# One change to a two-layer decoder trunk: where the third pooling group is multiplied, who adds and splits, and how the first and the down-projection loads are issued

## The chip, the cores and the metric

The kernel runs on one core of a Trainium2 chip. A core has a matrix engine (TensorE, PE in the profile, with its weight loads as PEld), a vector engine (VectorE, DVE), a scalar engine (ScalarE, ACT), GpSimd (POOL) and a queue that only issues loads and stores (SyncE, SP). They share an on-chip memory of 128 partitions, and TensorE's accumulation banks, of which this kernel uses eight of 128x512 float32. The metric is the device time of one execution in microseconds (us).

## The reference, cut to what matters

Two layers, 512 tokens, width 1024. Layer 0 mixes tokens by dilated attention, layer 1 by pooling; each is followed by a SwiGLU feed-forward network of width 2816, with a root-mean-square norm ahead of every part.

```python
def pooling_mixer(h, w_in, w_group, scale):
    u = (h @ w_in).reshape(B, S, POOL_GROUPS, POOL_GROUP_DIM)
    ys = [trailing_mean(u[:, :, g], w) - u[:, :, g] for g, w in enumerate(POOL_WINDOWS)]  # 2, 4, 8, 16
    y = jnp.einsum('bsgc,gcd->bsgd', jnp.stack(ys, axis=2), w_group).reshape(B, S, D_MODEL)
    return y * scale

def swiglu_ffn(h, w_gate_up, w_down):
    gu = h @ w_gate_up
    return (jax.nn.silu(gu[..., :D_FF]) * gu[..., D_FF:]) @ w_down

x = x + dilated_attention_mixer(rmsnorm(x, attn_norm), w_qkv, w_attn_out)
x = x + swiglu_ffn(rmsnorm(x, ffn_norm[0]), w_gate_up[0], w_down[0])
x = x + pooling_mixer(rmsnorm(x, pool_norm), w_pool_in, w_pool_group, pool_scale)
x = x + swiglu_ffn(rmsnorm(x, ffn_norm[1]), w_gate_up[1], w_down[1])
return rmsnorm(x, final_norm)
```

## The kernel before, in words

Activations lie transposed: X[0] to X[7] are eight tiles of 128 channels by 512 tokens. To keep float32 accuracy at TensorE's faster rate, every operand is split into a high half (a rounded copy) and a low half (the rest), and a product is three matmuls per chunk of 128 channels: high by high, high by low, low by high (lines 321, 322 and 324 for plain products; 453 to 455 in the seven-product scheme for 2x2 blocks that most of the work uses).

Weights stream through a ring of raw buffers. A plan that is written out ahead (lines 235 to 276) fixes the order of loads and splits, and `pump` works it off, behind each product. A plain weight unit is split in one of two ways (line 135). Either ScalarE makes the high half and VectorE subtracts (lines 91 and 92), or, if the unit is called `lean`, ScalarE makes the high half (L139) and its negation (L140), and GpSimd's queue adds the weights onto it by a second, accumulating load (L143). The first part (two chunks of the hidden width, `first == 0`) and the last part (four chunks) of each down projection are lean units of several pieces, each with a load of its own for every output chunk (L132 and L143).

The start (lines 887 to 919): the norms' weights are loaded, six warm-up matmuls on zeros run (L894, twelve passes in the profile), and for every chunk k of the input, X[k] (L902) and the first weights (L903) are loaded by SP, scaled and split (L383 or L385, L386; L908 or L906, L910), and multiplied in twelve matmuls (L914).

The pooling stage (lines 1219 to 1275) has four groups g of two chunks each. `pool(g)` takes two projections from TensorE, and on VectorE evacuates each (L1231), builds the window's sum (L1237 or L1241), subtracts (L1246, L1248) and splits the result (L91 on ScalarE, L92 on VectorE). `mix(g)` multiplies the two chunks by the group's weights in two products of six matmuls, adds the result to X (L1257), makes the next stage's operand (high half L385 on ScalarE, low half L386 on VectorE), squares X on ScalarE (L374) and adds the squares on GpSimd (L376). The order is pool 3, pool 2, mix 3, pool 1, mix 2, pool 0, mix 1, then the first products of the feed-forward network on chunks 4 to 7, then mix 0. Each projection is begun two calls ahead of its evacuation, so the last two are on TensorE while pool 1 is evacuated. Each engine works its own instructions strictly in the order in which they stand.

Of the kernel before, what the change touches and what calls it, by code (L numbers as in the profile page):

```python
# [9 lines left out]
F32R = mybir.dt.float32r  # L10
AF = mybir.ActivationFunctionType
OP = mybir.AluOpType
# [3 lines left out]
P = 128  # L16
# [20 lines left out]
NF = 4  # L37
H2 = S // 2
K2 = KC // 2
NPLAIN = 4  # L40
WARM = 6
NSOLO = 3
# [22 lines left out]
def trunk(ctx: ExitStack, tc: tile.TileContext, xT, xN, norms, w_first, w_qk, w_qkp, w_v0, w_v0p, w_v12, w_out, w_pair, w_down, w_dblock, w_pin, w_pgrp,  # L65
          consts, ident_in, invcnt_in, outT, outR):
    nc = tc.nc
# [52 lines left out]
    class Plain:  # L120


        def __init__(self, *srcs, shift=0, lean=False):
            self.srcs, self.n, self.w, self.shift, self.lean = srcs, sum(src.shape[-1] for src in srcs), None, shift, lean
            loads.append((self, {"raw": 1}, self.load))
            steps.append((self, "w", self.split))

        def load(self):
            self.raw = Held("raw")
            o = 0  # L130
            for src in self.srcs:
                nc.sync.dma_start(self.raw.t[:, o:o + src.shape[-1]], src)  # L132
                o += src.shape[-1]

        def split(self):
            self.w = Held("w", self.shift)
            hi, lo = (t[:, :self.n] for t in self.w.t)
            if self.lean:
                nc.scalar.activation(hi, self.raw.t[:, :self.n], AF.Copy)  # L139
                nc.scalar.activation(lo, hi.bitcast(F32), AF.Copy, scale=-1.0)  # L140
                o = 0
                for src in self.srcs:
                    nc.gpsimd.dma_start(lo[:, o:o + src.shape[-1]], src.bitcast(F32R), accum_op=OP.add)  # L143
                    o += src.shape[-1]
            else:
                split(hi, lo, self.raw.t[:, :self.n])
            self.raw.done()
# [103 lines left out]
    def ffn_plan(layer):  # L251
        j = 0
        for i, (first, end, block) in enumerate(PARTS):
# [10 lines left out]
            else:  # L264
                sizes = units_of(end - first)
                step = D // (sizes[0] * P) if len(sizes) == 1 else 1
                for m in range(0, KC, step):
                    o = first * P
                    for n in sizes:
                        share(step, *[w_down[layer, q, :, o:o + n * P] for q in range(m, m + step)], lean=True,  # L270
                              shift=LINE // 4 * (layer == 1 and end == FC and m + step > KC - ENDS))
                        o += n * P
# [86 lines left out]
    def give(key):  # L359
        del taken[held.pop(key)]  # L360
# [231 lines left out]
    with tc.tile_pool(name="opool", bufs=1) as opool:  # L592
        early = opool.tile([P, HEADS, S], F32R, tag="o", name="early")
        with tc.tile_pool(name="apool", bufs=1) as apool:
# [291 lines left out]

            nc.sync.dma_start(nrm, norms)
            lead = [Product(KC, stream(0), w=(None, None)) for i in range(NF)]
# [6 lines left out]
            for k in range(KC):  # L895
# [6 lines left out]
                nc.sync.dma_start(X[k], xT[:, k, :])  # L902
                nc.sync.dma_start(raw[:, s], w_first[k])  # L903
                if k:
                    scaled(0, k, *U[k])
                    nc.scalar.activation(hi[:, s], raw[:, s], AF.Copy)  # L906
                else:
                    nc.scalar.activation(hi[:, s], raw[:, s], AF.Copy)  # L908
                    scaled(0, k, *U[k], on_dve=True)
# [109 lines left out]
    with tc.tile_pool(name="fpool", bufs=2) as fpool:  # L1019
# [202 lines left out]

        def pool(g):
            Y[g] = []
            for c in range(2):
                left = KC - 2 * len(Y) - c + 2
                lead.extend(begin(min(left, 3) - len(lead), 2, range(KC)))
# [23 lines left out]
                split(*Y[g][-1], y)  # L1251

        def mix(g):
            for c in range(2):
                f = Product(2, lambda k: Y[g][k], w=wg[g // 2, g % 2]).add(range(2), pos=2 * c)
                m = 2 * g + c
# [3 lines left out]
                scaled(3, m, t[:, 0], t[:, 1])  # L1260
                square(3, m, nc.gpsimd)
            for c in range(2):
                give(("y", g, c))

        pool(3)
        pool(2)
        mix(3)
        pool(1)
        mix(2)
# [189 lines left out]
```

## Time and profile before

| | before |
|---|---|
| median of 3 runs | 1192.59 us (1192.28 to 1192.77) |
| the profiled execution's own time | 1192.39 us |
| its span in the profile | 1190.6 us |
| mean granted TensorE clock | 0.999 |
| moved from and to memory | 207.30 MB |

A row of the timeline has the start (us from the span's start), the duration, the engine, the line, the operation, what it writes and reads, how many alike are merged (x), and in brackets how long the engine had been idle and what ended that. A matmul's row runs to the end of its way through the array, so neighbouring rows overlap: what counts is the distance of two starts. A row of the waits names who waited, for whom, and three numbers: the total, how often, the longest.

### The profile page before, as it was taken

To read this page: it belongs to the slowest core of one execution; us is meant where nothing else is said; L and a number is where in the kernel's file an instruction comes from. 1 tells how busy PE (TensorE), PEld (TensorE's weight loads), DVE (VectorE), ACT (ScalarE), POOL (GpSimd) and SP (SyncE) were. 2 spreads that over 40 slices of the span, in tenths; PEclk is the share of its full clock that TensorE was granted. 3 is DMA by queue.
4 is the path that set the end of the run, shared out by engine and by line. 5 is a ranking of instruction groups with operands and counts; after the bars stand their busy time and mean duration, and the time that the engine had idled before them with its cause. 6 is when DMAs were issued, how large, how long until landed. Compare 5 with 4: busy or idle time off the path is not lost.

```text
span 1190.6 us, 24964 instructions
## 1 busy us (share of the span) xinstructions
PE 1180.9 (99%) x9936; PEld 1119.4 (94%) x9936; DVE 961.6 (81%) x1682; ACT 715.1 (60%) x1247; POOL 201.8 (17%) x201
## 2 busy tenths in 40 slices
PE   9999999999999999999999999999999999999997
PEld 7889999999999988889999999988789999999997
DVE  6978798889788854699988988657779998898855
ACT  6445564455456545747756776676575776676563
POOL 1111211111111002411111111122450111111120
PEclk9999999999999999999999999999999999999999
DMA  8346666665766548957777777798595777777763
GB/s 276 127 102 164 155 155 162 170 158 149 191 144 163 155 141 209 196 105 200 191 191 192 195 201 195 192 265 206 116 196 112 192 196 200 193 192 195 194 135 96
DMA packets 83733, 207.30 MB, mean 174 GB/s; under 512 B 8464, under 2 KB 13728, under 8 KB 83616
## 3 DMA queue, kind: packets, MB, share of 16 engines
q1 hardware_dynamic: 51552, 141.98, 36.3%
q0 software_dynamic: 31920, 63.46, 32.3%
q8 instruction: 78, 1.28, 0.4%
q14 instruction: 39, 0.32, 0.1%
q10 hardware_dynamic: 144, 0.26, 0.1%
HBM read 203.57 MB, written 2.10 MB: 173 GB/s over the span
## 4 chain that ended last, share of the span: by engine, by line
PE 97%; issue 1%; DVE 1%; ACT 1%; POOL 0%; DVEq 0%; POOLq 0%
PE ps L453 19%; PE ps L455 19%; PE ps L454 19%; PE ps L321 8%; PE ps L322 8%; PE ps L324 8%; PE ps L624 2%; PE ps L626 2%; PE ps L625 2%; PE ps L914 2%; PE ps L836 1%; PE ps L708 1%; PE ps L830 1%; PE ps L728 1%; PE ps L894 0%
## 5 line engine op out<-in xcount | busy, mean ns | idle before, releaser
L91 ACT ACTIVATE w<-raw 128x1024 fp32r<-128x1024 f32 x261 | 276.2, 1063 | 169.5 <-PE ps L455 71.8
L92 DVE TENSOR_TENSOR w<-raw,w 128x1024 fp32r<-128x1024 f32 x261 | 317.8, 1221 | 50.0 <-ACT w L91 46.0
L453 PE MATMUL ps<-far,w 128*128 128x256 f32 x896 | 246.7, 275 | 0.5 <-ACT first L527 0.5
L454 PE MATMUL ps<-far,w 128*128 128x256 f32 x896 | 246.5, 275 | 0.0
L455 PE MATMUL ps<-far,w 128*128 128x256 f32 x896 | 246.5, 275 | 0.0
L453 PE MATMUL ps<-near,w 128*128 128x256 f32 x640 | 180.3, 282 | 0.0
L454 PE MATMUL ps<-near,w 128*128 128x256 f32 x640 | 177.0, 277 | 0.0
L455 PE MATMUL ps<-near,w 128*128 128x256 f32 x640 | 176.9, 276 | 0.0
L453 PEld LDWEIGHTS ps<-far,w 128*128 128x128 f32 x896 | 168.2, 188 | 1.0 <-ACT first L527 0.9
L454 PEld LDWEIGHTS ps<-far,w 128*128 128x128 f32 x896 | 168.2, 188 | 0.1
L455 PEld LDWEIGHTS ps<-far,w 128*128 128x128 f32 x896 | 168.2, 188 | 0.0
L322 PE MATMUL ps<-near,w 128*128 128x512 f32 (+1 forms) x332 | 125.0, 377 | 1.3 <-DVE near L386 1.3
L321 PE MATMUL ps<-near,w 128*128 128x512 f32 (+1 forms) x332 | 125.6, 379 | 0.0
L324 PE MATMUL ps<-near,w 128*128 128x512 f32 (+1 forms) x332 | 124.9, 376 | 0.0
L453 PEld LDWEIGHTS ps<-near,w 128*128 128x128 f32 x640 | 120.5, 188 | 0.4
L454 PEld LDWEIGHTS ps<-near,w 128*128 128x128 f32 x640 | 120.3, 188 | 0.0
L455 PEld LDWEIGHTS ps<-near,w 128*128 128x128 f32 x640 | 120.3, 188 | 0.0
L168 POOL DMA_DIRECT2D raw<-w_pair x36 | 43.5, 1208 | 296.0 <-DMA raw<-w_pair 113.6
L322 PEld LDWEIGHTS ps<-near,w 128*128 128x128 f32 x332 | 62.4, 188 | 12.9 <-DVE near L386 1.7
L321 PEld LDWEIGHTS ps<-near,w 128*128 128x128 f32 x332 | 62.3, 188 | 11.7 <-ACT near L91 0.4
L324 PEld LDWEIGHTS ps<-near,w 128*128 128x128 f32 x332 | 62.3, 188 | 11.5
L139 ACT ACTIVATE w<-raw 128x1024 fp32r<-128x1024 f32 x36 | 37.8, 1056 | 37.4 <-PE ps L324 35.4
(311 smaller groups left out, 2813.1 us busy)
## 6 DMA issues: line engine op xcount, KB each, us to landing
raw<-w_pair SPq DMA_DIRECT2D x80, 512.0 KB, 4.9
raw<-w_qkp SPq DMA_DIRECT2D x36, 512.0 KB, 4.4
raw<-w_pair POOLq DMA_DIRECT2D x36, 512.0 KB, 7.5
raw<-w_dblock SPq DMA_DIRECT2D x32, 512.0 KB, 4.6
raw<-w_v SPq DMA_DIRECT2D x18, 512.0 KB, 4.3
raw<-w_qkp POOLq DMA_DIRECT2D x18, 512.0 KB, 7.5
rawhalf<-w_pair SPq DMA_DIRECT2D x36, 256.0 KB, 5.1
raw<-w_dblock POOLq DMA_DIRECT2D x16, 512.0 KB, 7.4
```

The source lines that it names most:

```text
L91: nc.scalar.activation(hi, v, AF.Copy)
L92: nc.vector.tensor_tensor(lo, v, hi.bitcast(F32), op=OP.subtract)
L139: nc.scalar.activation(hi, self.raw.t[:, :self.n], AF.Copy)
L168: nc.gpsimd.dma_start(self.b.rearrange("p (a c) -> p a c", a=2), self.src[:, None, 3 * n:].to_broadcast([P, 2, n]), accum_op=OP.add)
L321: nc.tensor.matmul(self.p[:, cols], w[0][:, s], mh[:, cols], start=self.done == 0, stop=False)
L322: nc.tensor.matmul(self.p[:, cols], w[0][:, s], ml[:, cols], start=False, stop=False)
L324: nc.tensor.matmul(self.p[:, cols], w[1][:, s], mh[:, cols], start=False, stop=self.done == self.n)
L453: nc.tensor.matmul(dst, w.t[0][:, c], th, start=k == 0 and not on, stop=False, skip_group_check=on)
L454: nc.tensor.matmul(dst, w.t[0][:, c], tl, start=False, stop=False, skip_group_check=on)
L455: nc.tensor.matmul(dst, w.t[1][:, c], th, start=False, stop=k == n - 1, skip_group_check=on)
L624: nc.tensor.matmul(o, mh, wh, start=k == 0, stop=False)
L625: nc.tensor.matmul(o, mh, wl, start=False, stop=False)
```

## The change

- At the start the norms are loaded by GpSimd's queue, four warm-up matmuls run instead of six, X[0] is SP's first load, and the first weights of chunk 0 come in two halves, each with a copy of its own on ScalarE.
- Units of several pieces are loaded by one transfer: four pieces of 256 columns or two of 512. The last part of layer 1's down projection is no longer lean: VectorE subtracts, and the accumulating loads there go.
- The two products of the pooling group g=2 are issued inside pool 1, between the last two projections; the rest of mix 2 follows pool 1 as before.
- In `mix` the squares are added by VectorE, both behind the two chunks' operands.

```diff
-WARM = 6
+WARM = 4
...
+        def views(self, t):
+            o = 0
+            for src in self.srcs:
+                q = src.shape[1] if len(src.shape) == 3 else 1
+                v = t[:, o:o + q * src.shape[-1]]
+                yield v.rearrange("p (q c) -> p q c", q=q) if len(src.shape) == 3 else v, src
+                o += q * src.shape[-1]
...
-                        share(step, *[w_down[layer, q, :, o:o + n * P] for q in range(m, m + step)], lean=True,
+                        share(step, w_down[layer, m:m + step, :, o:o + n * P].rearrange("q p c -> p q c"), lean=layer == 0 or first == 0,
...
-            nc.sync.dma_start(nrm, norms)
+            nc.gpsimd.dma_start(nrm, norms)
...
                 nc.sync.dma_start(X[k], xT[:, k, :])
-                nc.sync.dma_start(raw[:, s], w_first[k])
                 if k:
+                    nc.sync.dma_start(raw[:, s], w_first[k])
                     scaled(0, k, *U[k])
                     nc.scalar.activation(hi[:, s], raw[:, s], AF.Copy)
                 else:
-                    nc.scalar.activation(hi[:, s], raw[:, s], AF.Copy)
+                    for e in range(2):
+                        c = slice(e * NF * P // 2, (e + 1) * NF * P // 2)
+                        nc.sync.dma_start(raw[:, c], w_first[k][:, c])
+                        nc.scalar.activation(hi[:, c], raw[:, c], AF.Copy)
                     scaled(0, k, *U[k], on_dve=True)
...
-        def pool(g):
+        def pool(g, inside=None):
             Y[g] = []
             for c in range(2):
+                if inside and c:
+                    inside()
...
+        M = {}
+
+        def mixed(g):
+            M[g] = [Product(2, lambda k: Y[g][k], w=wg[g // 2, g % 2]).add(range(2), pos=2 * c) for c in range(2)]
+
         def mix(g):
-            for c in range(2):
-                f = Product(2, lambda k: Y[g][k], w=wg[g // 2, g % 2]).add(range(2), pos=2 * c)
+            if g not in M:
+                mixed(g)
+            for c, f in enumerate(M.pop(g)):
...
-                square(3, m, nc.gpsimd)
             for c in range(2):
+                square(3, 2 * g + c)
                 give(("y", g, c))
...
-        pool(1)
+        pool(1, lambda: mixed(2))
```

The first place is VectorE's program in the pooling stage, before the change, from the evacuation of the last projection on (`s_` with a number is a running sum, `x` the residual, `near` the next stage's operand, `far` a split pooled chunk):

```order
L1231 TENSOR_TENSOR u<-ps,row 128x512
L1237 TENSOR_TENSOR s_10273<-u 128x512
L1257 SCALAR_TENSOR_TENSOR x<-ps,nrm,x 128x512
L1244 TENSOR_TENSOR mean<-s_10273,invcnt 128x2
L1246 SCALAR_TENSOR_TENSOR u<-s_10273,u 128x510
L1257 SCALAR_TENSOR_TENSOR x<-ps,nrm,x 128x512
L386 SCALAR_TENSOR_TENSOR near<-x,nrm,near 128x512
L92 TENSOR_TENSOR far<-u,far 128x512
L386 SCALAR_TENSOR_TENSOR near<-x,nrm,near 128x512
```

After the change, from the evacuation of the last projection but one on (the changed file's lines 1240, 1246, 1253, 1255, 1257, 1272, 390 and 380 are lines 1231, 1237, 1244, 1246, 1248, 1257, 386 and 376 of before):

```order
L1240 TENSOR_TENSOR u<-ps,row 128x512
L1246 TENSOR_TENSOR s_10238<-u 128x512
L1272 SCALAR_TENSOR_TENSOR x<-ps,nrm,x 128x512
L1253 TENSOR_TENSOR mean<-s_10238,invcnt 128x2
L1255 SCALAR_TENSOR_TENSOR u<-s_10238,u 128x510
L1272 SCALAR_TENSOR_TENSOR x<-ps,nrm,x 128x512
L390 SCALAR_TENSOR_TENSOR near<-x,nrm,near 128x512
L380 TENSOR_TENSOR sq<-sq 128x512
L390 SCALAR_TENSOR_TENSOR near<-x,nrm,near 128x512
L380 TENSOR_TENSOR sq<-sq 128x512
L1257 TENSOR_TENSOR u<-mean,u 128x2
L92 TENSOR_TENSOR far<-u,far 128x512
```

The same chain of g=2 has moved from behind the last evacuation to behind the one before it, and two additions of squares stand in it.

The second place is ScalarE's program at the last gate and up pairs of layer 1, before the change (`w` is a weight buffer, `gt` the gate, `up` the gated chunk, `first` and `sums` copies out of the accumulation banks):

```order
L543 COPY sums<-ps 128x256
L139 ACTIVATE w<-raw 128x1024
L140 ACTIVATE w<-w 128x1024
L139 ACTIVATE w<-raw 128x1024
L1137 ACTIVATE gt<-gt 128x512
L140 ACTIVATE w<-w 128x1024
L91 ACTIVATE near<-up 128x512
L527 COPY first<-ps 128x256
```

And after it (lines 547, 1144, 531 and 535 are lines 543, 1137, 527 and 531 of before):

```order
L547 COPY sums<-ps 128x256
L91 ACTIVATE w<-raw 128x1024 x2
L1144 ACTIVATE gt<-gt 128x512
L531 COPY first<-ps 128x256
L91 ACTIVATE near<-up 128x512
L535 COPY sums<-ps 128x256
```

The negations are gone, and the copy that begins the next pair stands ahead of the split of `up`.

The third place is SP's program at the start, before and after the change (lines 906, 914 and 908 of the changed file load X, the halves and the other first weights):

```order
L887 DMA nrm<-norms 128x48
L902 DMA x<-xT 128x512
L903 DMA raw<-w_first 128x512
L902 DMA x<-xT 128x512
L903 DMA raw<-w_first 128x512
```

```order
L906 DMA x<-xT 128x512
L914 DMA raw<-w_first 128x256 x2
L906 DMA x<-xT 128x512
L908 DMA raw<-w_first 128x512
L906 DMA x<-xT 128x512
```

The norms have left this queue, and the second chunk is the fourth load in both.

More of the change, by code (lines that the diff above doesn't have):

```diff
@@ L123, in __init__ @@
         def __init__(self, *srcs, shift=0, lean=False):
[L124 removed]
+            self.srcs, self.n, self.w, self.shift, self.lean = srcs, sum(src.shape[-1] * (src.shape[1] if len(src.shape) == 3 else 1) for src in srcs), None, shift, lean
             loads.append((self, {"raw": 1}, self.load))
             steps.append((self, "w", self.split))
+        def views(self, t):
[5 more added lines that the diff above has]
+                o += q * src.shape[-1]
         def load(self):
             self.raw = Held("raw")
[L130 to L133, printed above, removed]
+            for v, src in self.views(self.raw.t):
+                nc.sync.dma_start(v, src)
         def split(self):
@@ L140, in split @@
                 nc.scalar.activation(lo, hi.bitcast(F32), AF.Copy, scale=-1.0)
[L141 to L144, printed above, removed]
+                for v, src in self.views(lo):
+                    nc.gpsimd.dma_start(v, src.bitcast(F32R), accum_op=OP.add)
             else:
```

## Prediction

> **What bounds the kernel now.** I read the page's engine table first, then the list of what TensorE waited for, then single rows of the timeline at those waits.
>
> ```profile
> PE 1180.9 (99%) x9936; PEld 1119.4 (94%) x9936; DVE 961.6 (81%) x1682; ACT 715.1 (60%) x1247; POOL 201.8 (17%) x201
> PE ps L322 <- DVE near L386: 1.3, 1, 1.3
> PE ps L894 <- DVE idle L891: 1.2, 1, 1.2
> PE ps L453 <- ACT first L527: 0.5, 2, 0.3
> ```
>
> TensorE is busy for 99% of the span, and the change takes no real product from it. So the change can only be worth what TensorE loses in waits, plus what passes before its first real product. The list is complete and short: one wait of 1.3 us for VectorE's L386, two of 0.3 us for ScalarE's L527, and the start. Everything else that the change touches lies beside a busy TensorE. I therefore price three places and cost the rest at nothing.
>
> **Part 1: the third group's product, and squares on VectorE.** The rows of TensorE at the longest wait:
>
> ```profile
> 849.73 0.39 PE L321 MATMUL ps<-near,w 128*128 128x512 f32 x1
> ...
> 850.41 0.39 PE L321 MATMUL ps<-near,w 128*128 128x512 f32 x1
> 852.05 0.50 PE L322 MATMUL ps<-near,w 128*128 128x512 f32 x1 [1.26 <-DVE near L386]
> 852.38 0.39 PE L324 MATMUL ps<-near,w 128*128 128x512 f32 x1
> ```
>
> VectorE there and ahead of it:
>
> ```profile
> 826.93 0.69 DVE L92 TENSOR_TENSOR far<-u,far 128x512 fp32r<-128x512 f32 x1 [0.63 <-ACT far L91]
> ...
> 839.05 0.69 DVE L1231 TENSOR_TENSOR u<-ps,row 128x512 f32<-128x512 f32 x1 [0.19 <-PE ps L324]
> ...
> 844.49 0.69 DVE L1231 TENSOR_TENSOR u<-ps,row 128x512 f32<-128x512 f32 x1 [3.16 <-PE ps L324]
> ...
> 847.88 0.74 DVE L386 SCALAR_TENSOR_TENSOR near<-x,nrm,near 128x512 fp32r<-128x512 f32 x1
> 848.54 1.78 DVE L92 TENSOR_TENSOR far<-u,far 128x512 fp32r<-128x512 f32 x1
> 850.24 1.76 DVE L386 SCALAR_TENSOR_TENSOR near<-x,nrm,near 128x512 fp32r<-128x512 f32 x1
> ```
>
> GpSimd's additions beside it, and the same addition by VectorE in another stage:
>
> ```profile
> 848.44 3.00 POOL L376 TENSOR_TENSOR sq<-sq 128x512 f32<-128x512 f32 x2 [0.45 <-ACT sq L374]
> 1165.49 0.69 DVE L376 TENSOR_TENSOR sq<-sq 128x512 f32<-128x512 f32 x1 [1.00 <-ACT sq L374]
> ```
>
> Undisturbed products of this shape start (850.41 - 849.73)/3 = 0.227 us apart. From 850.41 to 852.05 are 1.64 us, so 1.41 are lost, and the restart takes 0.33 instead of 0.227, another 0.10: **1.51 us**. The product that waits needs the low half of chunk 5 of the next stage's operand. L386 makes it, and it is late twice over: the third group (g=2) is multiplied only after the last projection, so its chain on VectorE begins after 844.49; and the two instructions beside GpSimd's additions (848.44 to 851.44) take 1.78 and 1.76 us where 0.69 and 0.74 are the rule.
>
> After the change TensorE does the two products of g=2 between the last two projections. Six matmuls each, 6 x 0.227 = 1.36 us from about 838.85 (just ahead of the evacuation at 839.05), give 840.2 and 841.6. The last projection moves back by the same 2.72 us, and the work behind starts where it did, at 849.73. The pooled input of g=2 was split by 827.6 (the row at 826.93), so the product waits for nothing. On VectorE the walk in its new order, with 0.69 us an instruction, is: evacuation 839.05, running sum 839.8, X[4] 840.5, window 841.2, X[5] 841.9, low half of 4 at 842.5 (ScalarE's high half is ready), addition, low half of 5 at 843.9 to 844.6. TensorE wants that at about 850.6: six microseconds of margin. The squares add seven additions, 7 x 0.69 = 4.8 us, to VectorE, which is paid from the 3.16 us of idle time in the row at 844.49 and from the stretched instructions. Behind the last group the margin is smallest: the low half of chunk 0 follows X[0] and X[1], ends near 859.5 and is wanted 24 + 12 + 13 matmuls after 849.73, at 860.8, so 1.3 us. The sum of squares is complete near 861.6 and wanted eleven matmuls on, at 863.3. So I take the whole 1.51; the bounds are 0 (the wait appears elsewhere in the stage) and 1.51.
>
> **Part 2: the last down projection of layer 1 split by VectorE.** TensorE at the second wait:
>
> ```profile
> 1150.58 0.28 PE L455 MATMUL ps<-far,w 128*128 128x256 f32 x1
> 1151.12 0.38 PE L453 MATMUL ps<-far,w 128*128 128x256 f32 x1 [0.27 <-ACT first L527]
> 1151.35 0.28 PE L454 MATMUL ps<-far,w 128*128 128x256 f32 x1
> ```
>
> ScalarE ahead of it:
>
> ```profile
> 1147.79 1.04 ACT L139 ACTIVATE w<-raw 128x1024 fp32r<-128x1024 f32 x1
> 1148.74 0.61 ACT L1137 ACTIVATE gt<-gt 128x512 f32<-128x512 f32 x1
> 1149.26 1.04 ACT L140 ACTIVATE w<-w 128x1024 fp32r<-128x1024 f32 x1
> 1150.20 0.61 ACT L91 ACTIVATE near<-up 128x512 fp32r<-128x512 f32 x1
> 1150.72 0.35 ACT L527 COPY first<-ps 128x256 f32<-128x256 f32 x1
> ```
>
> VectorE: the price of a subtraction, and the last split of `up`:
>
> ```profile
> 1145.18 1.23 DVE L92 TENSOR_TENSOR w<-raw,w 128x1024 fp32r<-128x1024 f32 x1 [0.67 <-ACT w L91]
> ...
> 1160.66 0.69 DVE L92 TENSOR_TENSOR near<-up,near 128x512 fp32r<-128x512 f32 x1 [0.70 <-ACT near L91]
> ```
>
> Here the spacing is 0.113. From 1150.58 to 1151.12 are 0.54, so 0.43 lost, and 0.12 in the restart: **0.54 us**. ScalarE ran without a gap into the copy that TensorE wanted. Without the two negations (1.04 us each by the row at 1149.26) and with the copy ahead of the split of `up`, the copy can run when its accumulation ends: twelve products (1.36 us) ahead of 1150.69, so about 1149.4, and it is done by 1149.9; TensorE wants it at 1150.69. VectorE gets four subtractions of 1.23 us; the second ends near 1149.6, which delays the gate's last quarter by 1.2 us and the activation hardly, because ScalarE is free earlier. At the next pair the same count puts the split of `up` at 1160.7, where it ended at 1161.35; with TensorE 0.54 earlier it is wanted from about 1161.7 (the last chunk's first product started at 1162.24). The eight accumulating loads on GpSimd's queue go away, off the path. Layer 0's equal wait stays, since its last part keeps the negations. Bounds: 0 and 0.54; I take 0.54.
>
> **Part 3: several chunks a transfer.** In the other down projections two or four loads become one with as many bytes. No row of TensorE's waits names a load of w_down, on either queue, so issues saved there are worth nothing. A later landing of the whole would cost only if it used up cover that TensorE has; none shows in the list. GpSimd's row for four such issues:
>
> ```profile
> 496.27 3.66 POOL L143 DMA_DIRECT2D w<-w_down  x4 [2.83 <-ACT w L140]
> ```
>
> What could be lost is that the first chunk now waits for the landing of the whole, three issues (2.7 us) later by this row; TensorE's gate and up products cover that, and no wait in the list is near. What stands behind on the two queues, the loads of the gate's pairs, is issued earlier. Zero, with 2.7 us at a place as the other end if that cover were gone.
>
> **Part 4: the start.**
>
> ```profile
> 1.24 5.49 PE L894 MATMUL ps<-idle 128*128 128x256 f32 x12 [1.24 <-DVE idle L891]
> 6.16 0.94 PE L914 MATMUL ps<-early,w 128*128 128x512 f32 x1
> 6.16 1.17 PE L914 MATMUL ps<-early,w 128*128 128x512 f32 x2
> 6.16 6.20 PE L914 MATMUL ps<-early,w 128*128 128x512 f32 x24
> ```
>
> ScalarE and VectorE at the first chunk, and ScalarE at the third:
>
> ```profile
> 4.49 0.63 ACT L374 ACTIVATE sq<-x 128x512 f32<-128x512 f32 x1 [2.27 <-DMA x<-xT]
> 4.57 0.49 DVE L383 TENSOR_SCALAR early<-x,nrm 128x512 fp32r<-128x512 f32 x1 [3.39 <-DMA x<-xT]
> 5.15 0.63 ACT L908 ACTIVATE w<-raw 128x512 fp32r<-128x512 f32 x1
> ...
> 10.14 0.72 ACT L385 ACTIVATE early<-x,nrm 128x512 fp32r<-128x512 f32 x1 [1.81 <-DMA x<-xT]
> 11.29 0.62 ACT L906 ACTIVATE w<-raw 128x512 fp32r<-128x512 f32 x1
> ```
>
> The first two loads on SP's queue, and a small load on GpSimd's (its time to landing last):
>
> ```profile
> 0.73 0.38 SPq L887 DMA_DIRECT2D nrm<-norms  x1
> 1.16 0.42 SPq L902 DMA_DIRECT2D x<-xT  x1
> ...
> invcnt<-invcnt_in POOLq DMA_DIRECT2D x1, 8.0 KB, 4.2
> ```
>
> Six warm-up matmuls are twelve passes, 5.49/12 = 0.46 us each; two fewer free TensorE at 6.73 - 1.83 = 4.90. The first chunk is issued at 0.73 instead of 1.16 and should be used from 4.06 instead of 4.49. The square (0.63) stands ahead of the weights on ScalarE, then two halves at 0.37 (the 128x256 copy above takes 0.35): first half 5.1. The norms now come by GpSimd's queue. Their nearest row there is the 4.2 us of `invcnt`: 4.93, so the operand ends near 5.5; if they are as quick as the first chunk, 4.6. The first product then starts between 5.1 and 5.6; I take 5.35.
>
> Before, the first product ends at 6.16 + 0.94 = 7.10 and the last warm-up pass at 6.73, so it cost about 0.4 us, where 0.227 is full pace; the second starts at 6.16 + 1.17 - 0.39 = 6.94 at full pace. Full pace so came 5.7 us after the warm-ups began, which ran without a hole. [...] The sum below goes by the rows alone, with full pace again at 6.94. Until then a product costs about 0.42. From 5.35 to 6.94 pass 3.8 products instead of one: a lead of 2.8 x 0.227 = 0.63 us. But it cannot all be kept. The 24 products of the first two chunks end so that the 25th starts at 12.36 - 0.39 + 0.23 = 12.20, and its weights are ready at 11.91: about 0.25 can be used with no load earlier. The rest needs the third chunk's load (awaited at 10.14) to land earlier. It is issued no earlier, but 0.43 us less lies ahead of it in the transfers' share; against that stand smaller pieces for the first weights. I take 0.2: **0.45 us**, with bounds 0.2 and 0.63.
>
> **Sum:** 1.51 + 0.54 + 0 + 0.45 = 2.50 us. The profiled execution took 1192.39 us, 1.79 around its span of 1190.6, and is 0.20 below the median of 1192.59. From its own time 1189.9; as a median, which I predict, 1192.59 - 2.50 = **1190.1 us**.
>
> **Rivals.**
> - *The clock.* A hole of about 0.45 us now lies between 4.90 and 5.35. If the count begins again there, full pace comes at 11.05; 13.6 products are done by then instead of 19.1, and 5.5 x 0.227 = 1.25 us are lost: 1192.59 - 2.05 + 1.25 = 1191.8. For it speaks that the slow stretch is that long; against it, that the 1.41 us hole at 850.41 left the pace as it was (852.38 follows after 0.33). Chance 0.12.
> - *The stage gains nothing.* VectorE, with 4.8 us more, becomes late for another operand (the 1.3 us margin is the place): 1192.59 - 0.54 - 0.45 = 1191.6. Against it stands that no addition then runs on GpSimd beside it. Chance 0.09.
> - *The norms land late*, and the kernel is slower. All of the first products need them. GpSimd's first load on its queue is not shown so early, and its loads can take long:
>
> ```profile
> DMA to landing us min/median/max: 4.1/7.2/13.9
> ```
>
> These are the accumulating loads of L143. At 13.9 the norms land at 14.6, the first product starts at 15.2 instead of 6.5, and 1192.59 - 2.05 + 8.7 = 1199.2. It decides from a landing of about 10.3 us, when the start loses more than 2.05 + 2.39. The queues are empty then, which speaks against it. Chance 0.04.
>
> **How the numbers follow.** The forecast has chance 0.75 and its own range 1189.5 to 1190.8. A measurement of this kernel tells about 0.2% (2.39 us) from no change; below 1190.2 is faster. The forecast lies just beyond: 0.57 of its chance is faster, 0.18 within. The clock and the stage that gains nothing (0.21) lie within 0.2%, the norms (0.04) beyond on the other side. So faster 0.57, same 0.39, slower 0.04. The range 1189.4 to 1191.6 leaves out the norms, about half of the clock's case and the forecast's edges.
>
> **What would show it.** In the changed profile TensorE's waits lose L386 wholly and one of the two for L527; L92 and L386 in the pooling stage take about 0.7 us throughout; the first L914 starts near 5.35, and the 25th between 11.6 and 12.0. It is wrong if a wait for VectorE stands near 860, if products early on are 0.42 us apart beyond 7, or if L383 waits for the norms beyond 5.

## The result, and the profile after

On one chip, side by side, the changed kernel takes 1190.53 us (median of 22 runs, 1189.47 to 1193.27) and the kernel before 1192.16 us (22 runs, 1191.58 to 1193.37). The ratio is 0.9986, with a 95% interval of 0.998 to 0.9992: about 1.6 us less. That something changed is clear from the interval, but the gain is smaller than the 0.2% (2.39 us) from which the forecast counted a kernel as faster. The forecast was 1190.1. Two of its three terms are right; the third, the start, has the wrong sign, and the changed kernel's runs lie 3.8 us apart where those of before lie 1.8 apart.

The page of the changed kernel, engines with busy time, share of the span (1188.8 us) and instructions, and then the list of what TensorE waited for (total, times, longest):

```profile
PE 1179.8 (99%) x9932; PEld 1118.4 (94%) x9932; DVE 966.0 (81%) x1693; ACT 711.9 (60%) x1244; POOL 171.6 (14%) x171
```

```profile
PE ps L898 <- DVE idle L895: 1.2, 1, 1.2
PE ps L921 <- ACT w L910: 0.8, 1, 0.8
PE ps L921 <- DVE early L387: 0.4, 1, 0.4
PE ps L457 <- ACT first L531: 0.3, 1, 0.3
```

The 1.3 us wait for VectorE's L386 (now L390) is gone, and so is one of the two waits for ScalarE's L527 (now L531). Two waits are new, both for L921, which are the first products (L914 before). To see what each place is worth I follow one kind of row through both kernels: TensorE's small sums over the squares (L403 before, L407 after), which stand at the end of a stage. Kernel before:

```profile
28.61 0.43 PE L403 MATMUL ps<-ones,sq 128*32 128x1 f32 x32
...
807.50 0.43 PE L403 MATMUL ps<-ones,sq 128*32 128x1 f32 x32
864.99 0.43 PE L403 MATMUL ps<-ones,sq 128*32 128x1 f32 x32
1174.97 0.31 PE L403 MATMUL ps<-ones,total 128*32 128x1 f32 x16
```

The changed kernel:

```profile
29.38 0.43 PE L407 MATMUL ps<-ones,sq 128*32 128x1 f32 x32
...
808.30 0.43 PE L407 MATMUL ps<-ones,sq 128*32 128x1 f32 x32
864.22 0.43 PE L407 MATMUL ps<-ones,sq 128*32 128x1 f32 x32
1173.56 0.30 PE L407 MATMUL ps<-ones,total 128*32 128x1 f32 x16
```

Distances tell it. Up to the first row the changed kernel is 0.77 us later: that is the start, in one execution of each (three kernels below with one and the same start, e1, e9 and e10, lie up to 1.0 apart there). From the first row to 808 it loses 0.03 more. The pooling stage takes 55.92 us where it took 57.49: 1.57 gained. The stretch behind it takes 309.34 where it took 309.98: 0.64 gained, all of it ahead of the first product of the last down part (1156.72, where it was 1158.13).

VectorE in the pooling stage, the chain of the third group's operand in the changed kernel:

```profile
843.23 0.74 DVE L390 SCALAR_TENSOR_TENSOR near<-x,nrm,near 128x512 fp32r<-128x512 f32 x1
...
844.50 0.75 DVE L390 SCALAR_TENSOR_TENSOR near<-x,nrm,near 128x512 fp32r<-128x512 f32 x1
...
846.67 0.69 DVE L92 TENSOR_TENSOR far<-u,far 128x512 fp32r<-128x512 f32 x1 [0.76 <-ACT far L91]
```

L390 and L92 take 0.7 us where they took 1.76 and 1.78, and the low half of chunk 5 is done at 845.3, not at 852.

ScalarE's copy that TensorE had waited for in layer 1 (L527 at 1150.72 before):

```profile
1148.82 0.38 ACT L531 COPY first<-ps 128x256 f32<-128x256 f32 x1 [0.48 <-PE ps L459]
```

ScalarE now waits for TensorE there, and TensorE's products run on without a gap.

The start of the changed kernel, TensorE first, then ScalarE, then VectorE:

```profile
5.40 1.98 PE L921 MATMUL ps<-early,w 128*128 128x512 f32 x4 [0.38 <-DVE early L387]
10.07 0.50 PE L921 MATMUL ps<-early,w 128*128 128x512 f32 x1 [0.84 <-ACT w L910]
...
3.61 0.63 ACT L378 ACTIVATE sq<-x 128x512 f32<-128x512 f32 x1 [1.39 <-DMA x<-xT]
4.15 0.40 ACT L915 ACTIVATE w<-raw 128x256 fp32r<-128x256 f32 x1
5.42 0.42 ACT L915 ACTIVATE w<-raw 128x256 fp32r<-128x256 f32 x1 [0.87 <-DMA raw<-w_first]
8.26 0.72 ACT L389 ACTIVATE early<-x,nrm 128x512 fp32r<-128x512 f32 x1 [2.42 <-DMA x<-xT]
9.41 0.61 ACT L910 ACTIVATE w<-raw 128x512 fp32r<-128x512 f32 x1
...
4.77 0.49 DVE L387 TENSOR_SCALAR early<-x,nrm 128x512 fp32r<-128x512 f32 x1 [3.58 <-DMA nrm<-norms]
```

The first product starts at 5.40, as forecast (5.35). The second chunk is late. Its input and its weights before the change:

```profile
6.57 0.72 ACT L385 ACTIVATE early<-x,nrm 128x512 fp32r<-128x512 f32 x1 [0.79 <-DMA x<-xT]
...
7.72 0.62 ACT L906 ACTIVATE w<-raw 128x512 fp32r<-128x512 f32 x1
```

Now ScalarE waits 2.42 us for the input (L389 at 8.26), the weights are copied at 9.41, and TensorE, done with the first chunk's twelve products, stands still until 10.07.

### The profile page after: what moved, and what is told of

Read it like the earlier page. It is cut to its first block, busy times and chain, and to the rows that moved or that the text cites. A ratio compares the mean times of both kernels' runs of the same rounds, so it can differ in the third digit from the quotient of the medians.

```text
span 1188.8 us, 24883 instructions
## 1 busy us (share of the span) xinstructions
PE 1179.8 (99%) x9932; PEld 1118.4 (94%) x9932; DVE 966.0 (81%) x1693; ACT 711.9 (60%) x1244; POOL 171.6 (14%) x171
## 4 chain that ended last, share of the span: by engine, by line
PE 97%; issue 1%; ACT 1%; DMA 1%; DVE 0%; SPq 0%; POOL 0%; DVEq 0%; POOLq 0%; ACTq 0%
PE ps L457 20%; PE ps L459 19%; PE ps L458 19%; PE ps L325 9%; PE ps L326 8%; PE ps L328 8%; PE ps L628 2%; PE ps L630 2%; PE ps L629 2%; PE ps L921 2%; PE ps L840 1%; PE ps L712 1%; PE ps L732 1%; PE ps L834 1%; DMA x<-xT 1%
## 5 line engine op out<-in xcount | busy, mean ns | idle before, releaser
L91 ACT ACTIVATE w<-raw 128x1024 fp32r<-128x1024 f32 x265 | 280.5, 1063 | 171.3 <-PE ps L459 69.4
L92 DVE TENSOR_TENSOR w<-raw,w 128x1024 fp32r<-128x1024 f32 x265 | 323.0, 1222 | 52.2 <-ACT w L91 47.9
L328 PEld LDWEIGHTS ps<-near,w 128*128 128x128 f32 x332 | 62.4, 188 | 11.5
L325 PEld LDWEIGHTS ps<-near,w 128*128 128x128 f32 x332 | 62.3, 188 | 11.5 <-ACT near L91 0.4
L91 ACT ACTIVATE half<-rawhalf 128x512 fp32r<-128x512 f32 x81 | 51.0, 631 | 14.6 <-PE ps L459 12.5
```

The source lines that it names most:

```text
L91: nc.scalar.activation(hi, v, AF.Copy)
L92: nc.vector.tensor_tensor(lo, v, hi.bitcast(F32), op=OP.subtract)
L325: nc.tensor.matmul(self.p[:, cols], w[0][:, s], mh[:, cols], start=self.done == 0, stop=False)
L328: nc.tensor.matmul(self.p[:, cols], w[1][:, s], mh[:, cols], start=False, stop=self.done == self.n)
```

## The experiments

The theory behind them: parts 1 and 2 work as forecast, and the start loses what it was to gain. The rivals: the start's loss in that one execution is chance; or one edit of the start alone (the halves, the norms' queue, the shorter warm-up) is at fault. Two measures are used throughout: the median, and the time of the first row of sums (28.61 before, 29.38 after), which sees nothing but the start, but in one profiled execution alone.

**e1: without the start's edits.** Parts 1 to 3, with the old start.

```diff
-WARM = 4
+WARM = 6
-            nc.gpsimd.dma_start(nrm, norms)
+            nc.sync.dma_start(nrm, norms)
-                    for e in range(2):
-                        c = slice(e * NF * P // 2, (e + 1) * NF * P // 2)
-                        nc.sync.dma_start(raw[:, c], w_first[k][:, c])
-                        nc.scalar.activation(hi[:, c], raw[:, c], AF.Copy)
+                    nc.sync.dma_start(raw[:, s], w_first[k])
+                    nc.scalar.activation(hi[:, s], raw[:, s], AF.Copy)
```

> Parts 1 to 3 with the start of before: six warm-up matmuls, norms first on SP's queue, the first weights in one load. Theory A (the start of the change loses about 0.8 us in most executions, since the second chunk's first load lands late): parts 1 and 2 stay worth 1.57 + 0.64 us and about 0.4 more near the end, so 2.2 to 2.6 us below the kernel before, and 0.6 to 0.9 below the changed kernel. Theory B (the late landing in the profiled execution of the changed kernel is chance, and the start is worth my 0.45 in most executions): about 1.3 us below the kernel before, 0.4 above the changed kernel. In the trace both expect no wait for L386, and the first product near 6.2 as before.

Measured: 1189.79 us (1189.10 to 1190.16), beside 1192.44 for the kernel before; ratio 0.9977 (0.9968 to 0.9986). The sums in its timeline:

```profile
28.53 0.43 PE L407 MATMUL ps<-ones,sq 128*32 128x1 f32 x32
...
807.41 0.43 PE L407 MATMUL ps<-ones,sq 128*32 128x1 f32 x32
863.33 0.43 PE L407 MATMUL ps<-ones,sq 128*32 128x1 f32 x32
1172.67 0.31 PE L407 MATMUL ps<-ones,total 128*32 128x1 f32 x16
```

The stage takes 55.92 and the stretch behind it 309.34, to the hundredth what they take in the changed kernel. Up to 807 the distance to the kernel before is 0.08 to 0.12 throughout, and layer 0's down projections with their merged transfers lie in that stretch: **part 3 is worth nothing**, as forecast. Without the start's edits the kernel is 0.74 us faster than with them by the two medians, and 1.02 if each is taken from the kernel before beside it. That is what theory A says.

**e2: the start's edits alone**, on the kernel before.

> The kernel before with only the new start: four warm-up matmuls, norms on GpSimd's queue, the first weights in two halves. Theory A (the start loses): 0.5 to 0.9 us above the kernel before, with a wait of TensorE for the second chunk's weights near 10 and no such wait in the kernel before. Theory B (chance): 0.2 to 0.6 us below the kernel before. In both the waits for L386 and for L527 stay as in the kernel before.

Measured: 1192.86 us (1191.70 to 1193.82) beside 1192.44; ratio 1.0003 (0.9994 to 1.0011). The median is 0.42 above the kernel before, just short of theory A's 0.5 to 0.9, and the interval holds both a small gain and a small loss; a gain of 0.45 us (0.9996) is not excluded by this run alone. The wait near 10 is there, but short (0.2 us, at 9.31), and the first sums stand at 28.58, as in the kernel before. So the start's loss is not the same in every execution, and this run alone does not show it.

**e3: norms back on SP's queue** in the changed kernel (that line alone).

> The changed kernel with the norms' load as the first on SP's queue again; four warm-ups and the halved first weights stay. If the load on GpSimd's queue is what holds up the second chunk (its packets lie among those of the first loads): the second chunk's load lands near 6.5 to 7 as in the kernel before, the wait near 10 goes, and the time is 0.6 to 1 us below the changed kernel. If the halved weights are the cause: the wait stays, and the time is 0 to 0.4 us above the changed kernel, since all later loads are issued 0.43 later. If it is chance: 0.2 to 0.4 above.

Measured: 1190.23 us (ten runs from 1189.89 to 1190.98, and the profiled one at 1192.51) beside 1192.44; ratio 0.9984 (0.9975 to 0.9993). The wait stays, so the norms' queue does not cause it. The median is 0.3 below the changed kernel's, 0.6 if each is taken from the kernel before beside it, where this case was expected at 0 to 0.4 above; so this load may cost something under four warm-ups, which two sessions do not settle. The profiled execution is the worst of its runs, and shows how a single one can be so slow. TensorE's rows:

```profile
9.99 0.50 PE L921 MATMUL ps<-early,w 128*128 128x512 f32 x1 [1.75 <-ACT w L910]
10.79 2.59 PE L921 MATMUL ps<-early,w 128*128 128x512 f32 x7
12.76 2.54 PE L921 MATMUL ps<-early,w 128*128 128x512 f32 x6
14.46 2.89 PE L921 MATMUL ps<-early,w 128*128 128x512 f32 x11
```

Products ran 0.23 apart up to the wait, and again behind it; then, from 11.49, they stand 0.43 apart, six in 2.54 us. Behind the wait of 1.75 us the slow pace came back, some 1.5 us after TensorE had started again; the mean granted clock of this execution is 0.996, that of the other ten 0.998 or 0.999. That is what my clock rival was about, at another place than I had put it and behind a longer stop.

**e4: the first weights whole** in the changed kernel (one load and one copy; norms on GpSimd's queue and four warm-ups stay).

> The changed kernel with the first weights in one load and one copy; norms on GpSimd's queue and four warm-ups stay. If the halves are the cause (packets of half the size, one more issue of 0.4 us ahead of the second chunk): the second chunk lands near 7 or earlier, the wait near 10 goes, and the time is 0.6 to 1.2 us below the changed kernel. If the norms on GpSimd's queue are the cause: the wait stays and the time is within 0.3 us of the changed kernel. If it is chance: within 0.3 us as well, but with the wait there in one trace and not in another.

Measured: 1190.02 us (1188.80 to 1192.89) beside 1192.44; ratio 0.9986 (0.9977 to 0.9995). The second chunk's input is used at 6.05, not at 8.26, and the wait near 10 is gone: the halves are its cause. But the median is only 0.5 us lower, and the runs lie 4.1 us apart, so another cause remains. In this execution TensorE's first product waits 1.0 us for VectorE's L387, because the norms land only at 5.36 and four warm-ups do not reach so far.

**e5, e6, e7: each edit of the start alone**, on the kernel of e1.

```diff
-WARM = 6
+WARM = 4
```

> Parts 1 to 3 with the old order of loads, and of the start's edits only the four warm-up matmuls for six. The first weights are ready where the copy ended in the kernel without this edit (5.73), so the first product starts near 5.8 instead of 6.17, after a hole of about 0.9 us. If the shorter warm-up is harmless and the lead is lost again where the second or third chunk lands: 0 to 0.3 us below that kernel, and as narrow a spread (1 us). If the hole makes the slow stretch begin again, as behind the wait of 1.75 us in the run with the norms back on SP's queue: 0.8 to 1.5 us above it, with products 0.42 apart beyond 8.

Measured: 1191.03 us (1188.68 to 1191.84) beside 1192.32; ratio 0.9988 (0.9979 to 0.9997). That is 1.24 above e1, as the second case says. TensorE's rows:

```profile
5.76 0.79 PE L919 MATMUL ps<-early,w 128*128 128x512 f32 x1 [0.73 <-DVE early L390]
6.77 2.76 PE L919 MATMUL ps<-early,w 128*128 128x512 f32 x6
9.65 2.70 PE L919 MATMUL ps<-early,w 128*128 128x512 f32 x11
```

Six products in 2.76 us from 6.77, eleven in 2.70 from 9.65: full pace came only near 9.5. In e4's profiled execution the products ran at full pace at 6.79, where e5's stood some 0.43 apart:

```profile
6.79 2.68 PE L919 MATMUL ps<-early,w 128*128 128x512 f32 x11
```

e6 halves the first weights (the four lines of e1's diff, put back), with six warm-ups and the norms on SP's queue.

> Parts 1 to 3 with six warm-ups and norms first on SP's queue; of the start's edits only the first weights in two halves. If the halves push the pause in the landings ahead of the second chunk: its load lands between 7.4 and 8.3 instead of 6.4, TensorE waits 0.4 to 1.2 us for its weights near 9.5, and the time is 0.4 to 1.0 us above the kernel without this edit. If the pause falls where it likes: the second chunk lands near 6.9 (one issue later), no wait, and the time is within 0.2.

Measured: 1190.61 us (1189.74 to 1191.70) beside 1192.32; ratio 0.9986 (0.9977 to 0.9995); 0.82 above e1. ScalarE and TensorE:

```profile
8.54 0.72 ACT L389 ACTIVATE early<-x,nrm 128x512 fp32r<-128x512 f32 x1 [2.56 <-DMA x<-xT]
...
10.35 0.50 PE L921 MATMUL ps<-early,w 128*128 128x512 f32 x1 [1.52 <-ACT w L910]
10.69 2.68 PE L921 MATMUL ps<-early,w 128*128 128x512 f32 x11
```

The late second chunk comes from the halves alone. The profiled execution is the slowest of its eleven runs, and 0.44 us of that were lost elsewhere (its stretch from 864.47 to 1174.25 takes 309.78, not 309.34; it follows a wait of ScalarE of 1.77 us for a load of `w_pair`, until 1052.84). Here the slow pace did not come back behind the wait of 1.52 us (eleven products in 2.68).

e7 loads the norms by GpSimd's queue (the one line), with six warm-ups and whole weights.

> Parts 1 to 3 with six warm-ups and the first weights whole; of the start's edits only the norms' load on GpSimd's queue. If this load is what makes the times of the changed kernel spread over 3.8 us (it lands between 4.3 and 5.4 in the three traces that have it): times spread over 2 us or more here too, and the median is 0 to 0.5 us above the kernel without this edit, since the six warm-ups cover a landing up to 5.6. If the load is harmless: a spread of 1 us, and the median 0 to 0.3 below, since every later load is issued 0.43 earlier.

Measured: 1189.93 us (1189.28 to 1190.30) beside 1192.32; ratio 0.998 (0.9971 to 0.9989). That is within 0.14 of e1 by medians and as narrow: harmless. In this execution the norms were the last to land (VectorE's L387 starts at 5.65, waiting for them), and six warm-ups covered it but for some 0.1 us (the last pass ends at 6.16, the first product starts at 6.29). My suspicion that this load makes the times spread is refuted.

**e8: the other last part too.** On the kernel of e1, layer 0's last down part is split by VectorE as well.

```diff
-... lean=layer == 0 or first == 0,
+... lean=first == 0,
```

> Parts 1 to 3 with the old start, and the last down projection of layer 0 split by VectorE as well as that of layer 1. If that wait is like the one of layer 1 (0.64 gained there by the trace): the wait for L531 near 767 goes, 0.4 to 0.6 us below the kernel without this edit. If VectorE becomes late there, since the operand of the next stage is made right behind: a new wait for VectorE between 768 and 790, and the time within 0.2 or above.

Measured: **1188.29 us** (five runs, 1188.10 to 1188.64) beside 1192.32; ratio 0.9968 (0.9955 to 0.998). TensorE's list has one line left, the wait for the zeros of the warm-up:

```profile
PE ps L898 <- DVE idle L895: 1.2, 1, 1.2
```

Its sums stand at 480.68 and 805.94, those of e1 at 481.12 and 807.41: the stretch takes 325.26 where it took 326.29, so 1.03 us are gained there, twice what I had expected. 0.69 of it lie up to the first product of the last down part (773.18 against 774.31, less the 0.44 by which this execution is ahead already); most of the other third is a second, smaller delay that stood behind the wait, at 778.58 in e1:

```profile
778.19 0.39 PE L328 MATMUL ps<-near,w 128*128 128x512 f32 x1
778.58 0.97 PE L325 MATMUL ps<-near,w 128*128 128x512 f32 x3
779.38 0.42 PE L326 MATMUL ps<-near,w 128*128 128x512 f32 x1
```

The first distance is 0.39 and the three products then take 0.80, where 0.227 each is the rule, so 0.28 are lost; in e8 all products there are 0.23 apart. The product at 778.58 starts when ScalarE's split of `up` (L91) ends at 778.52, and that split stands 2.3 us earlier in e8. The list of waits did not show this second delay. By medians e8 is 1.5 us below e1; these 1.03 are the part that the traces locate.

**e9 and e10: the two halves of part 1**, on the kernel of e1. e9 leaves the product where it was; e10 leaves the squares on GpSimd.

```diff
-        pool(1, lambda: mixed(2))
+        pool(1)
```

> Parts 1 to 3 with the old start, but without the move of the third group's product: it stands behind the last projection as in the kernel before, and only the squares of the pooling stage are VectorE's. If the stretched pair on VectorE (1.78 and 1.76 where 0.7 is the rule, beside GpSimd's additions) was enough to make the wait: the operand is done near 850.0 by the clock of the kernel before and wanted at 850.6, so no wait for L390, and between the row sums at 807 and at 865 the trace gains the same 1.57 us as with both. If the late order of the work was the main cause: a wait of 0.5 to 1.3 us stays there, and the time is as much above the kernel with both.

```diff
                 scaled(3, m, t[:, 0], t[:, 1])
+                square(3, m, nc.gpsimd)
             for c in range(2):
-                square(3, 2 * g + c)
                 give(("y", g, c))
```

> Parts 1 to 3 with the old start, with the third group's product between the last two projections, but the squares of the pooling stage stay GpSimd's additions. If the late order was enough to make the wait: no wait for L390 near 850 and the same 1.57 us between the row sums at 807 and at 865. If GpSimd's additions beside VectorE matter: some L92 and L390 rows take 1.2 to 1.8 us, and where the margin is smallest, behind the last group near 860, a wait of 0.3 to 1.2 us appears; the time is as much above the kernel with both.

Measured: e9 1189.91 us (1188.98 to 1190.65), ratio 0.998 (0.9971 to 0.9989); e10 1189.89 us (1189.19 to 1190.41), ratio 0.9979 (0.997 to 0.9988); before 1192.31. The sums of e9, then of e10:

```profile
807.86 0.43 PE L407 MATMUL ps<-ones,sq 128*32 128x1 f32 x32
863.78 0.43 PE L407 MATMUL ps<-ones,sq 128*32 128x1 f32 x32
```

```profile
806.82 0.43 PE L407 MATMUL ps<-ones,sq 128*32 128x1 f32 x32
862.74 0.43 PE L407 MATMUL ps<-ones,sq 128*32 128x1 f32 x32
```

55.92 us in both: **either half alone takes the whole 1.57 us**, and the second adds nothing. In e10 VectorE is still stretched beside GpSimd, at a place where nobody waits for it:

```profile
851.22 1.78 DVE L390 SCALAR_TENSOR_TENSOR near<-x,nrm,near 128x512 fp32r<-128x512 f32 x1
```

**e11: two warm-ups**, and **e12: five**, the one on the kernel of e1, the other on that of e8. In the kernel before, with six, full pace came 5.7 us after the first one began, at 6.94; e11 asks whether it still does across a hole of some 2.6 us.

> Parts 1 to 3 with the old order of loads, but two warm-up matmuls instead of six: TensorE is idle from about 3.1 to 5.75. [...] If it is counted from the first matmul, whatever lies between: full pace near 7, and within 0.5 us of the kernel with six.

Measured: 1191.68 us (1190.76 to 1192.94) beside 1192.31; ratio 0.9995 (0.9985 to 1.0004); 1.9 above e1. Two rows of TensorE:

```profile
6.79 2.74 PE L919 MATMUL ps<-early,w 128*128 128x512 f32 x6
9.35 2.91 PE L919 MATMUL ps<-early,w 128*128 128x512 f32 x12
```

Full pace came near 9.4, 8.2 us after the warm-ups began and not near 7, in an execution in which TensorE was idle for 2.45 us ahead of the first product (at 5.77). That full pace is counted from the first matmul, whatever lies between, is refuted by this execution; what it does go by is not shown.

> The fastest kernel so far (parts 1 to 3, the old order of loads, both last down projections split by VectorE; 1188.29) with five warm-up matmuls for six: they end near 5.3, and the first product starts near 5.75 after a hole of 0.45 us. If holes under 0.6 us do no harm to the pace: within 0.3 us of that kernel, on the lower side, with a spread of 1 us. If any hole there lets the slow stretch begin again in part of the executions: a spread of 2 us or more and a median 0.5 to 1.2 us above.

Measured: 1188.52 us (five runs, 1187.96 to 1188.91) beside 1192.31; ratio 0.9967 (0.9954 to 0.9979), a spread of 1 us: no harm and no gain that could be told from e8. In its profiled execution full pace had come before the hole (the warm-up pass at 4.68 takes 0.38 us, where the changed kernel's last, at 4.39, takes 0.64), so it does not show what a hole of that size does to a pace that is still to rise.

All the kernels together (first sums: the row of L407 or L403 near 28, in the profiled execution; x1: when ScalarE starts on the second chunk, L389 or L385). The medians come from four sessions, in which the kernel before took 1192.16, 1192.44, 1192.32 and 1192.31, so rows of different sessions compare only to some 0.3 us:

| kernel | warm-ups | first weights | norms by | x1 | first sums | median us | lowest to highest |
|---|---|---|---|---|---|---|---|
| before (with e1) | 6 | whole | SP | 6.57 | 28.61 | 1192.44 | 1191.57 to 1193.26 |
| e2 | 4 | halves | GpSimd | 7.50 | 28.58 | 1192.86 | 1191.70 to 1193.82 |
| after | 4 | halves | GpSimd | 8.26 | 29.38 | 1190.53 | 1189.47 to 1193.27 |
| e3 | 4 | halves | SP | 8.17 | 30.88 | 1190.23 | 1189.89 to 1192.51 |
| e4 | 4 | whole | GpSimd | 6.05 | 27.98 | 1190.02 | 1188.80 to 1192.89 |
| e5 | 4 | whole | SP | 5.84 | 29.50 | 1191.03 | 1188.68 to 1191.84 |
| e6 | 6 | halves | SP | 8.54 | 29.62 | 1190.61 | 1189.74 to 1191.70 |
| e7 | 6 | whole | GpSimd | 6.28 | 28.24 | 1189.93 | 1189.28 to 1190.30 |
| e1 | 6 | whole | SP | 6.43 | 28.53 | 1189.79 | 1189.10 to 1190.16 |
| e9 | 6 | whole | SP | 6.43 | 28.98 | 1189.91 | 1188.98 to 1190.65 |
| e10 | 6 | whole | SP | 6.40 | 27.99 | 1189.89 | 1189.19 to 1190.41 |
| e11 | 2 | whole | SP | 6.82 | 29.42 | 1191.68 | 1190.76 to 1192.94 |
| e8 | 6 | whole | SP | 6.98 | 28.08 | 1188.29 | 1188.10 to 1188.64 |
| e12 | 5 | whole | SP | 5.88 | 27.85 | 1188.52 | 1187.96 to 1188.91 |

## Why the prediction was right, and where it was wrong

**Part 1, right.** 1.51 us were forecast, 1.57 measured, and the walk of VectorE's instructions stands in the trace nearly to the tenth (low half of chunk 5 forecast to end at 844.6, done at 845.3 with the start 0.8 late). I named two reasons why the operand was late; e9 and e10 show that each was enough. My margin of 1.3 us behind the last group held: no wait near 860. The forecast called the operand late twice over; that either cure would do was not in it.

**Part 2, right, a little small.** 0.54 forecast, 0.64 measured, as the distance between two rows of sums; this part was never run alone, and whether the missing negations or the copy's earlier place cured the wait was not told apart. The 0.10 more lie between the wait and 1158.13 (1156.72 after), where the products of before stand a little further apart than the rule. e8 shows how such an estimate can fall short by more: I had called the list of waits complete, and in layer 0 a delay of 0.28 follows the wait without a row in that list.

**Part 3, right.** Zero, by e1's distances up to 807.

**Part 4, wrong in sign.** A gain of 0.45 us (0.2 to 0.63) was forecast; by medians the start loses 0.7 to 1.0 (after against e1, in two sessions), 0.77 in the profiled execution, and 0.42 by e2, whose interval also holds a gain. The first product came at 5.40, as forecast, but the sign that I had named for the rest failed: the 25th product, forecast between 11.6 and 12.0, starts at 12.97, where it started at 12.20 before. Two steps failed.

The first is "the rest needs the third chunk's load to land earlier". I looked at the third chunk, because that was the late one before, and took the second as safe. With the halves the pause in the landings, which stood behind the second chunk before (ScalarE's L385 at 10.14 waiting for the third), stands ahead of it. In the four profiled executions with halves, the second chunk's input is used at 7.50 to 8.54; in the ten with whole weights at 5.84 to 6.98, and the two do not overlap. "Against that stand smaller pieces for the first weights" was the right worry, but it only took what was left of the lead (0.38) down to 0.2, where e6 measures a loss of 0.82 by itself. Why the pause moves is open: the loads were not changed one at a time any further.

The second is "full pace again at 6.94". That was one execution's moment. The warm-up passes of e8, then of e1:

```profile
3.54 2.26 PE L898 MATMUL ps<-idle 128*128 128x256 f32 x7
```

```profile
4.39 2.34 PE L898 MATMUL ps<-idle 128*128 128x256 f32 x5
```

Seven passes in 2.26 us in the one, five in 2.34 in the other: in e8 full pace came in their midst, near 4.7, in e1 behind them, near 6.8. In e6 it came near 5.3 and in e7 near 5.4, and with a hole it can be 9.4 or 9.5 (e11, e5). So a shorter warm-up is a lottery: e5's runs reach from 1188.68, below all of e1's, to 1191.84. The clock rival stood at 0.12 and in the profiled execution of the changed kernel it did not come true (full pace near 7.2, products 0.23 apart from there on); by itself (e5) it costs 1.24 at the median. What spoke against it in my text, the hole of 1.41 us at 850 that left the pace alone, was about losing full pace, not about reaching it. In the rival of the late norms, the 6.5 for the first product stands in no row (it was 6.16); that changes its time by 0.3 and no chance.

By medians the edits do not add up: alone, four warm-ups cost 1.24 and the halves 0.82, together in e3 only 0.44. In e3 the first half lets the products begin at 5.18, so the hole is short. Why e4, with a longer hole than e5, has a lower median (1190.02 against 1191.03) is not settled; both spread over 3 us or more.

**The sum.** Forecast were 2.50 us less than 1192.59; measured are 1.63 less than 1192.16, the median of before in the runs beside it, and so the time itself is off by only 0.4. That it is so near is in part luck: the start was off by 1.2 to 1.5 us, and what made up for most of it was a kernel before that took 0.43 less than the 1192.59 I had started from, and parts 1 to 3, which gave more than forecast. I had given 0.57 to a time below 1190.2; the measured one lies in the 0.39 above it. Parts 1 to 3 gave 2.65 us in e1, and 2.40 and 2.42 in e9 and e10, which leave out one half of part 1 each (each against its own runs of before), where 2.05 were forecast, and the start took back 0.7 to 1.0 of it. Of the excess of parts 1 to 3, 0.16 is in the trace (1.57 + 0.64 against 2.05). The rest is not located: the time from the last row of L403 or L407 (1182.67 before, 7.7 us behind the last one shown) to the end of the span is 7.9 us before, 7.7 in e1, 8.1 in e9 and 7.4 in e8, so single executions differ there by as much. A smaller loss of the shorter warm-up shows outside the span: between an execution's span and its time lie 1.72 to 1.88 us in every kernel with five or six warm-ups, and up to 2.06 to 2.94 in the six with four or two (2.90 in the changed kernel, 2.00 on average; 2.94 in e5). Why is open.

## What to carry to other kernels

Where a wait has two causes, either cure may be the whole cure: try them apart, and keep the cheaper. At a kernel's start, look at the next operand that lands, not at the one that was late before, and keep TensorE busy without a hole until its real work begins (four and two warm-ups instead of six cost 1.24 and 1.9 us at the median, e5 and e11). And a start is judged by its spread over many runs, since one profile shows one draw of the pace and of the landings.

## What the runs showed of the hardware

- Full pace did not come a fixed time after the first matmul. Warm-ups that began at 1.24 in every kernel reached it by 4.7 in e8 and e12 and near 7.2 in the changed kernel, and at 9.5 and 9.4 in e5 and e11. Ahead of the first product TensorE was idle for 0.38 us in the changed kernel, 0.73 in e5 and 2.45 in e11; but in e4, behind a wait of 1.0 us, eleven products from 6.79 on took 2.68 us, full pace, so the idle time alone does not tell the moment. What does is not shown.
- Full pace was lost behind a stop of 1.9 us (e3, from 8.07 to 9.99): the products stand 0.23 apart up to 11.49 and 0.43 from there to about 14.9, some 3.4 us. It was not lost behind one of 1.7 (e6) or 1.0 (after, from 9.07 to 10.07). One loss is all that this rests on, and why it came only at 11.5 is not shown.
- The first loads came with a pause in their landings. ScalarE waited for the second chunk in the changed kernel (2.42 us, until 8.26) and in e6 (2.56, until 8.54), for that chunk's weights in e9 (1.35, until 9.03) and for the third chunk before the change (1.81, until 10.14). Behind the pause SP issued loads of 256 KB 0.7 us apart (before, at 10.13, 10.82, 11.49 and 12.17). It was no fixed cost: before the change TensorE did not wait for the third chunk at all, in e9 it waited 0.2 us, in the changed kernel 0.84 and in e6 1.52.
- The norms' load of 24 KB took 3.0 to 4.3 us to land by GpSimd's queue (e2 and e7) and 1.8 by SP's (before). Under six warm-ups neither cost anything that the medians show; under four, the first product waited for it by 0.4 us (after) and 1.0 (e4).
- VectorE's L92 and L386 took up to 1.8 us instead of 0.7 beside GpSimd's additions (before, and e10, where L386 is L390), and 0.7 throughout the pooling stage where VectorE did the additions itself (after, e9).
